# A transformer block in front of a PEER block on one core: six instead of four blocks of queries taken from the unscaled sum, and three smaller moves in the order of work

## The chip, the core and the metric

The kernel runs on one core of a Trainium2 chip. The core has five engines with a queue of instructions each: TensorE (PE in the profile; its weight loads are PEld), VectorE (DVE), ScalarE (ACT), GpSimd (POOL) and SyncE (SP), which here only starts DMA transfers. They wait for each other through semaphores. The metric is device time in microseconds (us) of one execution. A difference under about 0.2% (2.8 us) can't be told from none.

## The reference

Two layers follow each other on 256 tokens of width 1024. The first has latent attention (8 heads), differential attention (4 heads, two softmax maps each, o1 - lambda * o2, normed) and a gated FFN. The second is modulated by a condition vector: pooling and attention over neighbours and a context, then a product-key expert layer (PEER). The parts around the change, cut down:

```python
o_diff = rmsnorm(o1 - lam * o2, diff_subln_g) * (1.0 - lambda_init)     # end of differential attention
...
hx = rmsnorm(x, norm1_g) * (1 + sc1) + sh1                              # h1: x is the first layer's output xb
zx = hx @ w_in                                                          # pooled part, queries, keys, values
x = x + g1 * (concat([pool_x, attn_x], -1) @ w_out)                     # x3; w_out is wo2 in the kernel
h2 = rmsnorm(x, norm2_g) * (1 + sc2) + sh2
q = (h2 @ w_q).reshape(tokens, 8 heads, 2, 128)                         # 16 blocks of 128 query columns
s = einsum('thpd,hpnd->thpn', q, sub_keys)                              # scores against 128 keys per half
sv, si = top_k(s, 16)                                                   # and the 16 best of 16 x 16 sums
a = gelu(h2 @ u.T at the chosen experts);  x = x + g2 * ((softmax * a) @ v)
```

All 16384 experts' products are computed densely and masked; the result is within float32 accuracy.

## The kernel before

Activations lie transposed: 128 columns of the width on the partitions, 256 tokens in the free dimension, 8 such pieces (k) for the width of 1024. To keep float32 accuracy at the speed of the fast float32 format, every operand is split in a high part, rounded (`...h`, `whi`, made by ACT at L133), and the rest (`...l`, `wlo`, made by DVE at L130). A product of a weight block with the activations (`mm3`, L166) is then, for each k, three matmuls: whi x high (L169), whi x low (L170), wlo x high (L171). A block of 128 output columns with K = 8 has 24 matmuls of 128 x 256. `Weights` loads 2048 columns of weights at a time (`raw`, three buffers, SP queue) and splits 1024 columns, one block, at a time (`whi` and `wlo`, three buffers each); a buffer comes free when the last matmul that reads it has run. `lin_t` runs over the output blocks and hands the accumulators (PSUM tiles psa to psd, two buffers each) to a function that empties them.

A scheduler orders each engine's instructions when the program is built: it takes an instruction that is ready by its own timing model, the earliest in program order first, `tc.high_priority()` ahead of others, and `tc.issue_after(x)` not before x. The engines then keep this order.

The places that matter here, in order of time:

- **Differential attention** (two passes of 128 queries, qb = 0 and 1) ends with sums, a norm and the split into `odh`, `odl` (L580, L581), which the branch product wbd reads.
- **h1** (`modulated`, L660): rows of the norm (`rb`) come by a matmul broadcast (`rows_of`, L255); for each k DVE multiplies (L662, tile mdt), ACT adds the shift and rounds (L664, L668 and L133), and DVE takes the rest (L665, L130). Then `xb`, the first layer's normed output, is formed in place from x2 by eight DVE rows (L726), behind the instruction that `modulated` returns.
- **wo2** (L827): 8 blocks read `cath`, `catl`, whose pieces 0 to 3 come from the pooling and 4 to 7 from the neighbour attention's last queries.
- **The queries of PEER.** The norm of x3 needs all of x3. So `put_x3` also stores x3 times the gain unscaled (`z3`, in the tiles kall0 and kall1, with two columns of the shift behind the 256 tokens, hence 128 x 258), and the first four of the 16 blocks of wq (accumulators `psz`, two psa and two psb) are multiplied from z3; the norm's factor and the shift are applied when they are emptied (`put_pq`, L885, L886, with `rb4s`, an SBUF copy of the factor's row, and the shift's product in `sh4`). Between them stand the sum of squares (L246), GpSimd's power -1/2 (L215), the broadcast (L255) and `modulated` for h2. The other 12 blocks are multiplied from h2.
- **The search.** Each pair of query blocks is multiplied with the keys (L893), copied (`sc`, L895), and searched on DVE (`top16`, L873 to L877, and the sums' search); after all heads of 128 tokens the indices are picked out (tile eq, L955 to L967). All this is issued in pieces (`feed`) beside the dense product of h2 with u (`u_pass`), whose weight blocks need their wlo from the same DVE queue.

```python
psz = [f()[:, :S + 2] for f in (ps_a, ps_a, ps_b, ps_b)]
mm3(psz[0], wq, 0, KD, z3)
with tc.high_priority(), tc.issue_after(last_mm[0].ins):
    y4 = rsqrt_cols(ss3.done(), 1.0 / D)
mm3(psz[1], wq, KD, KD, z3)
with tc.high_priority(), tc.issue_after(last_mm[0].ins):
    rb4 = rows_of(y4)
    modulated(x3, rb4, gs2, lambda k: mod[:, 24 + k:25 + k], h2h, h2l)
for i in (2, 3):
    with tc.issue_after(last_bc[0].ins):
        mm3(psz[i], wq, i * KD, KD, z3)
```

Of the kernel before, what the change touches and what calls it, by code (L numbers as in the profile page):

```python
# [63 lines left out]
def block_kernel(ctx: ExitStack, tc: tile.TileContext, a: dict, out: bass.AP, dbg=None):  # L64
# [19 lines left out]
    def ps_a(name="psa"):  # L84
        return bank("a", name)
# [46 lines left out]
    def split(dst_h, dst_l, src, eng="v"):  # L132
        nc.scalar.activation(dst_h, src, AF.Copy)  # L133
        sub(eng, dst_l, src, dst_h)
# [28 lines left out]
            o = b % 8 * P  # L163
            return self.hl[0][:, o:o + n * P], self.hl[1][:, o:o + n * P]

    def mm3(ps, w, b, K, xs):  # L166
        for k in range(K):
            wh, wl = w(b + k)
            nc.tensor.matmul(ps, wh, xs[0][:, k], start=(k == 0), stop=False)  # L169
            nc.tensor.matmul(ps, wh, xs[1][:, k], start=False, stop=False)  # L170
            last_mm[0] = nc.tensor.matmul(ps, wl, xs[0][:, k], start=False, stop=(k == K - 1))  # L171
# [350 lines left out]
    def pv(pts, vh, o):  # L522
        for kb, p_ in enumerate(pts):
            nc.tensor.matmul(o, p_, vh(kb), start=(kb == 0), stop=(kb == len(pts) - 1))
# [28 lines left out]
    for qb in range(2):  # L553
        o1, o2 = ps_d(), ps_d()
        z = small.tile([P, 4, 2], F32, tag="dz", name="dz")
        for h0 in (0, 2):
            for e, o in enumerate((o1, o2)):
                ptss = soft([[(dq[64 * e:64 * e + 64, h], dk[64 * e:64 * e + 64, h])] for h in (h0, h0 + 1)], qb,
                            [z[:, h, e:e + 1] for h in (h0, h0 + 1)])
                for h, pts in zip((h0, h0 + 1), ptss):  # L560
                    pv(pts, lambda kb: dv[:, kb, h * 128:(h + 1) * 128], o[:, h * 128:(h + 1) * 128])
        r = small.tile([P, 4, 2], F32, tag="dr", name="dr")
        nc.vector.reciprocal(r, z)
        nc.vector.tensor_scalar(r[:, :, 1], r[:, :, 1], nlam, None, op0=OP.mult)
# [14 lines left out]
        oh, ol = (x[:, :, qb * P:(qb + 1) * P] for x in (odh, odl))  # L579
        nc.scalar.activation(oh, pv_, AF.Copy, scale=subg)  # L580
        nc.vector.scalar_tensor_tensor(ol, pv_, subg, oh.bitcast(F32), op0=OP.mult, op1=OP.subtract)  # L581

    st1a.close()

# [74 lines left out]
    def modulated(src, rb, gs, sh, hi, lo):  # L659
        for k in range(KD):  # L660
            t = mdp.tile([P, S], F32, tag="mdt", name="mdt")
            nc.vector.scalar_tensor_tensor(t, src[:, k], gs[:, k:k + 1], rb, op0=OP.mult, op1=OP.mult)  # L662
            if k % 2 == 0:
                nc.scalar.activation(hi[:, k], t, AF.Identity, bias=sh(k))  # L664
                end = nc.vector.scalar_tensor_tensor(lo[:, k], t, sh(k), hi[:, k].bitcast(F32),  # L665
                                                     op0=OP.add, op1=OP.subtract)
            else:
                nc.scalar.activation(t, t, AF.Identity, bias=sh(k))  # L668
                split(hi[:, k], lo[:, k], t)
        return end  # L670


# [151 lines left out]
        nc.vector.scalar_tensor_tensor(zl, x3[:, k], g, zh.bitcast(F32), op0=OP.mult, op1=OP.subtract)  # L824
        ss3.add(x3[:, k])

    lin_t(a["wo2"], 8, KD, (cath, catl), put_x3, grp=1)  # L827
    tap("x3", x3)
    shift = mod[:, 24:32, None].to_broadcast([P, KD, 2])
    split(z3[0][:, :, S:], z3[1][:, :, S:], shift)  # L830
    wq = Weights(a["wq"])
    psz = [f()[:, :S + 2] for f in (ps_a, ps_a, ps_b, ps_b)]

    h2h = acts.tile([P, KD, S], F32R, tag="acth", name="h2h")
    h2l = acts.tile([P, KD, S], F32R, tag="actl", name="h2l")
# [1 line left out]
    with tc.high_priority(), tc.issue_after(last_mm[0].ins):  # L837
        y4 = rsqrt_cols(ss3.done(), 1.0 / D)
    mm3(psz[1], wq, KD, KD, z3)
    with tc.high_priority(), tc.issue_after(last_mm[0].ins):  # L840
        rb4 = rows_of(y4)
        modulated(x3, rb4, gs2, lambda k: mod[:, 24 + k:25 + k], h2h, h2l)
    for i in (2, 3):
        with tc.issue_after(last_bc[0].ins):
            mm3(psz[i], wq, i * KD, KD, z3)
    h2 = (h2h, h2l)
# [31 lines left out]

    def put_pq(h2_, n, ps):
        pq = tk.tile([P, 2, S], F32, tag="pq", bufs=3, name="pq")  # L880
        if h2_ < 4:
            for i in range(2):
                z_ = psz[h2_ + i]
                nc.scalar.activation(sh4[:, h2_ + i:h2_ + i + 1], z_[:, S:S + 1], AF.Copy)
# [150 lines left out]

    rb4s = tk.tile([P, S], F32, name="rb4s")
    nc.scalar.activation(rb4s, rb4, AF.Copy)
    sh4 = tk.tile([P, 4], F32, name="sh4")
    for j in (0, 2):
        put_pq(j, 2, None)  # L1040
    lin_t(a["wq"], 16, KD, h2, put_pq, w=wq, j0=4)

    def u_pass(q):
        w = Weights(a["uT"][:, q * QJ * D:(q + 1) * QJ * D])
# [235 lines left out]
```

## Time and profile before

| | |
|---|---|
| median of 3 runs | 1380.24 us (1377.74 to 1380.52) |
| the profiled execution | 1381.32 us, of which its span 1379.1 us |
| PE, PEld | 98%, 91% of the span busy |
| DVE, ACT, POOL | 73%, 51%, 1% |
| mean granted TensorE clock | 0.994 of full speed |
| DMA | 217 GB/s over the span |

The span runs from the first to the last instruction of the profile. The busy share is time in which an engine ran at least one instruction; where an engine is nearly always busy, the little that it waits is what the order of work can still change.

### The profile page before, as it was taken

To read this page: it belongs to the slowest core of one execution; us is meant where nothing else is said; L and a number is where in the kernel's file an instruction comes from. 1 tells how busy PE (TensorE), PEld (TensorE's weight loads), DVE (VectorE), ACT (ScalarE), POOL (GpSimd) and SP (SyncE) were. 2 spreads that over 40 slices of the span, in tenths; PEclk is the share of its full clock that TensorE was granted. 3 is DMA by queue.
4 is the path that set the end of the run, shared out by engine and by line. 5 is a ranking of instruction groups with operands and counts; after the bars stand their busy time and mean duration, and the time that the engine had idled before them with its cause. 6 is when DMAs were issued, how large, how long until landed. Compare 5 with 4: busy or idle time off the path is not lost.

```text
span 1379.1 us, 24018 instructions
## 1 busy us (share of the span) xinstructions
PE 1349.9 (98%) x9736; PEld 1255.9 (91%) x9736; DVE 1013.3 (73%) x1746; ACT 708.1 (51%) x1034; POOL 20.0 (1%) x23
## 2 busy tenths in 40 slices
PE   7999999999999999899999999999999999999997
PEld 7988999999998888899999999999998888888886
DVE  5897679997988556699994998844466666677675
ACT  5564645454546555545454555544444554454443
POOL 0000000000000001000000000000000000000000
PEclk9999999999999999999999999999999999999999
DMA  6474348877885622354555678775566776778772
GB/s 238 150 249 152 107 139 298 282 275 259 284 312 203 217 93 81 138 180 158 182 196 181 238 272 296 291 274 200 196 231 228 242 250 237 263 271 285 242 236 87
DMA packets 82093, 300.44 MB, mean 218 GB/s; under 512 B 5824, under 2 KB 39232, under 8 KB 52800
## 3 DMA queue, kind: packets, MB, share of 16 engines
q1 hardware_dynamic: 76224, 274.02, 57.5%
q10 hardware_dynamic: 5760, 24.91, 4.5%
q8 instruction: 76, 1.25, 0.3%
q14 instruction: 33, 0.27, 0.1%
HBM read 276.88 MB, written 22.02 MB: 217 GB/s over the span
## 4 chain that ended last, share of the span: by engine, by line
PE 89%; DVE 5%; DMA 3%; issue 2%; ACT 1%; POOL 0%; SPq 0%; POOLq 0%; DVEq 0%; ACTq 0%
PE acc L1096 25%; PE psc L169 9%; PE psc L171 9%; PE psc L170 9%; PE psa L170 8%; PE psa L171 8%; PE psa L169 8%; DMA aw<-in_ada 3%; DVE wlo L130 2%; PE psd L1012 1%; PE psb L1012 1%; PE psd L774 1%; PE psb L505 1%; PE psb L762 1%; DVE jk L304 1%
## 5 line engine op out<-in xcount | busy, mean ns | idle before, releaser
L133 ACT ACTIVATE whi<-raw 128x1024 fp32r<-128x1024 f32 (+1 forms) x426 | 448.4, 1053 | 491.5 <-PE psc L170 176.2
L130 DVE TENSOR_TENSOR wlo<-raw,whi 128x1024 fp32r<-128x1024 f32 (+1 forms) x426 | 518.3, 1219 | 217.3 <-ACT whi L133 216.2
L169 PE MATMUL psc<-h2h,whi 128*128 128x256 f32 x1024 | 290.9, 284 | 0.0
L171 PE MATMUL psc<-h2h,wlo 128*128 128x256 f32 x1024 | 289.8, 284 | 0.0
L170 PE MATMUL psc<-h2l,whi 128*128 128x256 f32 x1024 | 289.6, 283 | 0.0
L170 PEld LDWEIGHTS psc<-h2l,whi 128*128 128x128 f32 x1024 | 196.4, 192 | 0.0
L169 PEld LDWEIGHTS psc<-h2h,whi 128*128 128x128 f32 x1024 | 196.3, 192 | 0.0
L171 PEld LDWEIGHTS psc<-h2h,wlo 128*128 128x128 f32 x1024 | 196.1, 192 | 0.0
L1096 PE MATMUL acc<-wlo,wgh 128*128 128x512 f32 x512 | 159.9, 392 | 0.8 <-DVE wlo L130 0.8
L1096 PE MATMUL acc<-whi,wgl 128*128 128x512 f32 x512 | 158.9, 389 | 0.0
L1096 PE MATMUL acc<-whi,wgh 128*128 128x512 f32 x512 | 139.6, 390 | 0.0
L1096 PEld LDWEIGHTS acc<-whi,wgl 128*128 128x128 f32 x512 | 96.1, 188 | 20.1
L1096 PEld LDWEIGHTS acc<-whi,wgh 128*128 128x128 f32 x512 | 95.8, 188 | 20.2 <-ACT whi L133 0.2
L1096 PEld LDWEIGHTS acc<-wlo,wgh 128*128 128x128 f32 x512 | 95.1, 188 | 20.4 <-DVE wlo L130 1.1
L171 PE MATMUL psa<-acth,wlo 128*128 128x256 f32 x352 | 99.8, 284 | 0.6 <-DVE wlo L130 0.6
L169 PE MATMUL psa<-acth,whi 128*128 128x256 f32 x352 | 99.8, 283 | 0.1
L170 PE MATMUL psa<-actl,whi 128*128 128x256 f32 x352 | 99.6, 283 | 0.0
L169 PE MATMUL psa<-xh,whi 128*128 128x256 f32 x240 | 70.9, 295 | 7.1 <-ACT whi L133 6.4
L170 PE MATMUL psa<-xl,whi 128*128 128x256 f32 x240 | 70.9, 296 | 0.7 <-DVE xl L332 0.7
L171 PE MATMUL psa<-xh,wlo 128*128 128x256 f32 x240 | 70.9, 296 | 0.0
L171 PEld LDWEIGHTS psa<-acth,wlo 128*128 128x128 f32 x352 | 67.6, 192 | 0.8 <-DVE wlo L130 0.8
L169 PEld LDWEIGHTS psa<-acth,whi 128*128 128x128 f32 x352 | 67.6, 192 | 0.3 <-DVE xT L614 0.3
(416 smaller groups left out, 2437.9 us busy)
## 6 DMA issues: line engine op xcount, KB each, us to landing
raw<-in_uT SPq DMA_DIRECT2D x64, 1024.0 KB, 4.9
raw<-in_v SPq DMA_DIRECT2D x64, 1024.0 KB, 4.9
aw<-in_ada SPq DMA_DIRECT2D x48, 512.0 KB, 5.8
raw<-in_wgu SPq DMA_DIRECT2D x22, 1024.0 KB, 4.8
ggd<-gs ACTq DMA_DIRECT2D x16, 1024.0 KB, 5.2
gh<-ggd SPq DMA_DIRECT2D x16, 1024.0 KB, 8.1
raw<-in_wA SPq DMA_DIRECT2D x14, 1024.0 KB, 4.9
raw<-in_wdn SPq DMA_DIRECT2D x11, 1024.0 KB, 7.2
```

The lines of the kernel that those rows point to most:

```text
L130: e.tensor_tensor(dst, src, hi.bitcast(F32), op=OP.subtract)
L133: nc.scalar.activation(dst_h, src, AF.Copy)
L169: nc.tensor.matmul(ps, wh, xs[0][:, k], start=(k == 0), stop=False)
L170: nc.tensor.matmul(ps, wh, xs[1][:, k], start=False, stop=False)
L171: last_mm[0] = nc.tensor.matmul(ps, wl, xs[0][:, k], start=False, stop=(k == K - 1))
L304: nc.vector.scalar_tensor_tensor(jk, aw, 1.0, c_, op0=OP.mult, op1=OP.mult, accum_out=dst[:, t:t + 1])
L505: nc.tensor.matmul(s[:, i], q_[:, qb * P:(qb + 1) * P], k_[:, :n], start=(j == 0), stop=False)
L762: nc.tensor.matmul(s, q2[x_][hd, hp, qs_], kall[y_][hd, hp], start=(i == 0), stop=(i == 2))
L774: nc.tensor.matmul(o[:, h * 64:(h + 1) * 64], pts[:, kb * P:(kb + 1) * P], v2[:, kb, h * 64:(h + 1) * 64], start=(kb == 0), stop=(kb == 3))
L1012: nc.tensor.matmul(ps[:, t4 * P:(t4 + 1) * P], o1[:, 2 * g4 + t4 // 2, :, t4 % 2], og[:, c, 2 * g4 + t4 // 2, :, t4 % 2], start=(c == 1), ...
L1096: r = nc.tensor.matmul(acc[tt][n], x_, w_[:, n * 512:(n + 1) * 512], start=st, stop=sp)
```

## The change

Four moves:

1. Six blocks of wq, not four, are multiplied from z3 (`NZ = 6`, the two more in psc buffers), so ten are left for h2. Half of block 2 (k = 0 to 3) is issued before the broadcast, the other half and blocks 3 to 5 behind it.
2. `modulated` returns the last low half of k = 7 instead of that of k = 6, so what is placed behind it (xb) stands behind all of h1. Its odd pieces are written out, with the same operations as `split`.
3. wo2's first two blocks are issued as k = 0 to 3 of both, then k = 4 to 7 of both.
4. The end of differential attention for qb = 1 is issued under `tc.high_priority()`.

```diff
+    def held(w, b):
+        hi, lo = w(b, 8)
+        return lambda c: (hi[:, (c - b) * P:(c - b + 1) * P], lo[:, (c - b) * P:(c - b + 1) * P])
+
-    def mm3(ps, w, b, K, xs):
-        for k in range(K):
+    def mm3(ps, w, b, K, xs, ks=None):
+        for k in ks or range(K):
...
+        hurry = ExitStack()
+        if qb == 1:
+            hurry.enter_context(tc.high_priority())
         r = small.tile([P, 4, 2], F32, tag="dr", name="dr")
...
         nc.vector.scalar_tensor_tensor(ol, pv_, subg, oh.bitcast(F32), op0=OP.mult, op1=OP.subtract)
+        hurry.close()
...
-                end = nc.vector.scalar_tensor_tensor(lo[:, k], t, sh(k), hi[:, k].bitcast(F32),
-                                                     op0=OP.add, op1=OP.subtract)
+                nc.vector.scalar_tensor_tensor(lo[:, k], t, sh(k), hi[:, k].bitcast(F32),
+                                               op0=OP.add, op1=OP.subtract)
             else:
                 nc.scalar.activation(t, t, AF.Identity, bias=sh(k))
-                split(hi[:, k], lo[:, k], t)
+                nc.scalar.activation(hi[:, k], t, AF.Copy)
+                end = nc.vector.tensor_tensor(lo[:, k], t, hi[:, k].bitcast(F32), op=OP.subtract)
...
-    lin_t(a["wo2"], 8, KD, (cath, catl), put_x3, grp=1)
+    wo2 = Weights(a["wo2"])
+    first = [(ps_a(), held(wo2, j * KD), j) for j in range(2)]
+    for ks in (range(4), range(4, KD)):
+        for ps, w_, j in first:
+            mm3(ps[:, :S], w_, j * KD, KD, (cath, catl), ks)
+    for ps, _, j in first:
+        put_x3(j, 1, ps[:, None, :S])
+    lin_t(a["wo2"], 8, KD, (cath, catl), put_x3, grp=1, w=wo2, j0=2)
...
-    psz = [f()[:, :S + 2] for f in (ps_a, ps_a, ps_b, ps_b)]
+    NZ = 6
+    psz = [f()[:, :S + 2] for f in (ps_a, ps_a, ps_b, ps_b, ps_c, ps_c)]
...
-    with tc.high_priority(), tc.issue_after(last_mm[0].ins):
+    mm3(psz[2], wq, 2 * KD, KD, z3, range(4))
+    end = last_mm[0]
+    with tc.high_priority(), tc.issue_after(end.ins):
         rb4 = rows_of(y4)
         modulated(x3, rb4, gs2, lambda k: mod[:, 24 + k:25 + k], h2h, h2l)
-    for i in (2, 3):
+    with tc.issue_after(last_bc[0].ins):
+        mm3(psz[2], wq, 2 * KD, KD, z3, range(4, KD))
+    for i in range(3, NZ):
         with tc.issue_after(last_bc[0].ins):
             mm3(psz[i], wq, i * KD, KD, z3)
...
-        if h2_ < 4:
+        if h2_ < NZ:
...
-    for j in (0, 2):
+    for j in range(0, NZ, 2):
         put_pq(j, 2, None)
-    lin_t(a["wq"], 16, KD, h2, put_pq, w=wq, j0=4)
+    lin_t(a["wq"], 16, KD, h2, put_pq, w=wq, j0=NZ)
```

What the scheduler makes of it is seen in the order of each engine's instructions. On PE, around the sum of squares of x3 (psd_5996) and the broadcast of its root (ny), before (psb_6287 is the accumulator of block 2):

```order
L246 MATMUL psd_5996<-cst_76,sq_6281 128x1
L170 MATMUL psa_6286<-kall1_4832,whi_6329 128x258
L171 MATMUL psa_6286<-kall0_4831,wlo_6330 128x258
L255 MATMUL psd_6357<-cst_76,ny_6325 128x128 x2
L169 MATMUL psb_6287<-kall0_4831,whi_6398 128x258
L170 MATMUL psb_6287<-kall1_4832,whi_6398 128x258
L171 MATMUL psb_6287<-kall0_4831,wlo_6399 128x258
```

and in the changed program, where L251 is the sum, L260 the broadcast, L174 to L176 the three matmuls, and the "..." stands for nine more rows of psb_6287:

```order
L251 MATMUL psd_5996<-cst_76,sq_6281 128x1
L175 MATMUL psa_6286<-kall1_4832,whi_6331 128x258
L176 MATMUL psa_6286<-kall0_4831,wlo_6332 128x258
L174 MATMUL psb_6287<-kall0_4831,whi_6361 128x258
L175 MATMUL psb_6287<-kall1_4832,whi_6361 128x258
L176 MATMUL psb_6287<-kall0_4831,wlo_6362 128x258
...
L260 MATMUL psd_6377<-cst_76,ny_6327 128x128 x2
```

Twelve matmuls of block 2 moved ahead of the broadcast. Behind it stand the other twelve, then 24 each into psb_6288, psc_6289 and psc_6290, and then the first matmul on h2h.

On DVE at the end of h1, before (h1l is the low half of h1, xT holds x2 and then xb, wlo_5163, wlo_5191 and wlo_5224 belong to the first three blocks that are multiplied with h1):

```order
L665 SCALAR_TENSOR_TENSOR h1l_5101<-mdt_5129,mod_79,h1h_5100 128x256
L726 SCALAR_TENSOR_TENSOR xT_75<-xT_75,cols_73,rbf_5141 128x256 x4
L130 TENSOR_TENSOR h1l_5101<-mdt_5124,h1h_5100 128x256
L726 SCALAR_TENSOR_TENSOR xT_75<-xT_75,cols_73,rbf_5141 128x256 x4
L130 TENSOR_TENSOR wlo_5191<-raw_5160,whi_5190 128x1024
L130 TENSOR_TENSOR h1l_5101<-mdt_5133,h1h_5100 128x256
L130 TENSOR_TENSOR wlo_5224<-raw_5221,whi_5223 128x1024
```

and in the changed program:

```order
L674 SCALAR_TENSOR_TENSOR h1l_5101<-mdt_5129,mod_79,h1h_5100 128x256
L679 TENSOR_TENSOR h1l_5101<-mdt_5124,h1h_5100 128x256
L130 TENSOR_TENSOR wlo_5191<-raw_5160,whi_5190 128x1024
L679 TENSOR_TENSOR h1l_5101<-mdt_5133,h1h_5100 128x256
L736 SCALAR_TENSOR_TENSOR xT_75<-xT_75,cols_73,rbf_5141 128x256 x8
L130 TENSOR_TENSOR wlo_5224<-raw_5221,whi_5223 128x1024
```

The eight rows of xb moved behind the last two low halves and ahead of wlo_5224.

On DVE in the first `u_pass`, beside the search, before (eq picks indices; wlo_7556 is the low half of the weight block that PE takes at 658 us of the profile):

```order
L130 TENSOR_TENSOR wlo_7507<-raw_7476,whi_7506 128x1024
L950 TENSOR_TENSOR ij_7541<-ijt_7542 128x128
L960 TENSOR_TENSOR eq_7549<-eq_7549,sf_7473 128x2048
L876 MAX sv_8067<-s2_8068 128x8
L876 MAX sv_8067<-s2_8074 128x8
L874 MAX_INDEX ti_7756<-tv_7755,cd_7997 128x8
L875 MATCH_REPLACE cd2_7998<-tv_7755,cd_7997 128x80
L874 MAX_INDEX si_7757<-sv_8150,sc4_6483 128x8 x2
L130 TENSOR_TENSOR wlo_7556<-raw_7553,whi_7555 128x1024
```

and in the changed program, where the same block's low half is wlo_7562:

```order
L130 TENSOR_TENSOR wlo_7513<-raw_7482,whi_7512 128x1024
L897 MATCH_REPLACE s2_8074<-sv_8073,sc3_6542 128x128
L897 MATCH_REPLACE s2_8080<-sv_8073,sc3_6542 128x128
L895 MAX tv_7761<-cd_8003 128x8
L895 MAX sv_8156<-sc4_6543 128x8 x2
L899 MAX_INDEX ti_7762<-tv_7761,cd2_7921 128x8
L972 TENSOR_TENSOR ij_7547<-ijt_7548 128x128
L982 TENSOR_TENSOR eq_7555<-eq_7555,sf_7479 128x2048
L130 TENSOR_TENSOR wlo_7562<-raw_7559,whi_7561 128x1024
```

The six short rows between eq and the low half moved behind it; and over the whole stretch from the first row of the search (MAX of sc0) to this low half the changed queue holds two rows of L130 fewer, since two more blocks of wq are split before the search begins. For moves 3 and 4 the rows of all engines stand as before, apart from line numbers and buffer numbers. On SP one load of w2 stands ahead of that of row_icnt, the counts of the pooling, no longer behind it.

## Rows read from the trace of the kernel before

**Rows 1.** The page, busy time, share of the span and instructions of each engine.

```profile
PE 1349.9 (98%) x9736; PEld 1255.9 (91%) x9736; DVE 1013.3 (73%) x1746; ACT 708.1 (51%) x1034; POOL 20.0 (1%) x23
```

**Rows 2.** Timeline of PE, pauses: start, us, instruction, idle before, releaser.

```profile
183.20 0.50 PE L169 MATMUL psa<-odh,whi 128*128 128x256 f32 x2 [1.22 <-ACT odh L580]
184.54 0.39 PE L170 MATMUL psa<-odl,whi 128*128 128x256 f32 x1 [0.84 <-DVE odl L581]
...
446.60 0.39 PE L170 MATMUL psa<-h1l,whi 128*128 128x256 f32 x1 [1.21 <-DVE h1l L130]
...
563.15 0.71 PE L255 MATMUL psd<-cst,ny 128*128 128x128 f32 x4 [1.78 <-POOL ny L215]
...
574.56 0.35 PE L169 MATMUL psa<-h2h,whi 128*128 128x256 f32 x1 [3.44 <-DVE pq L885]
```

**Rows 3.** Stretches: length, busy time of each engine, granted clock, DMA share, GB/s.

```profile
core 0 of [0], span 1379.1 us
...
182.00:188.00 6.00, 3.96 (x23) 3.76 (x24) 2.16 (x3) 1.14 (x2) 0.00 (x0) 0.82 0.51 175
446.00:450.00 4.00, 3.40 (x28) 3.40 (x29) 2.91 (x4) 1.17 (x2) 0.00 (x0) 1.00 0.99 373
562.00:566.00 4.00, 2.85 (x19) 2.85 (x20) 3.77 (x8) 2.04 (x6) 1.09 (x1) 0.84 0.63 209
566.00:570.00 4.00, 4.00 (x28) 4.00 (x28) 2.27 (x5) 1.93 (x6) 0.00 (x0) 0.74 0.13 53
574.00:578.00 4.00, 3.44 (x17) 3.47 (x18) 1.94 (x7) 1.71 (x4) 0.00 (x0) 0.62 0.13 53
578.00:582.00 4.00, 4.00 (x36) 4.00 (x35) 1.28 (x10) 1.62 (x3) 0.00 (x0) 0.96 0.01 4
588.00:594.00 6.00, 6.00 (x53) 6.00 (x52) 6.00 (x32) 2.90 (x4) 0.00 (x0) 1.00 0.60 214
```

**Rows 4.** Timeline of PE, blocks 2 and 3 from the unscaled sum.

```profile
565.07 0.42 PE L170 MATMUL psb<-kall,whi 128*128 128x258 f32 x1
...
567.64 0.42 PE L170 MATMUL psb<-kall,whi 128*128 128x258 f32 x1
...
568.22 0.28 PE L170 MATMUL psb<-kall,whi 128*128 128x258 f32 x1
...
570.84 0.28 PE L171 MATMUL psb<-kall,wlo 128*128 128x258 f32 x1
```

**Rows 5.** Timeline of DVE and ACT between the broadcast and the first scores.

```profile
563.90 1.66 DVE L662 SCALAR_TENSOR_TENSOR mdt<-xT,gs,psd 128x256 f32<-128x256 f32 x4 [0.23 <-PE psd L255]
...
568.10 1.06 ACT L133 ACTIVATE whi<-raw 128x1024 fp32r<-128x1024 f32 x1 [2.07 <-PE psb L170]
...
573.15 0.37 ACT L1037 ACTIVATE rb4s<-psd 128x256 f32<-128x256 f32 x1
...
574.00 0.75 DVE L885 TENSOR_TENSOR pq<-psa,rb4s 128x256 f32<-128x256 f32 x2
...
580.09 0.60 ACT L895 ACTIVATE sc<-psd 128x512 f32<-128x512 f32 x1 [3.93 <-PE psd L893]
...
580.72 0.49 DVE L873 MAX8 sv<-sc 128x8 f32<-128x128 f32 x2 [4.78 <-ACT sc L895]
```

**Rows 6.** Timeline of PE and DVE at the end of h1.

```profile
442.25 0.39 PE L169 MATMUL psa<-h1h,whi 128*128 128x256 f32 x1
...
443.41 1.67 DVE L726 SCALAR_TENSOR_TENSOR xT<-xT,cols,rbf 128x256 f32<-128x256 f32 x4
...
446.12 0.42 DVE L130 TENSOR_TENSOR h1l<-mdt,h1h 128x256 fp32r<-128x256 f32 x1
446.46 1.23 DVE L130 TENSOR_TENSOR wlo<-raw,whi 128x1024 fp32r<-128x1024 f32 x1
```

**Rows 7.** Timeline of DVE and PE in the first dense pass.

```profile
653.41 2.29 DVE L960 TENSOR_TENSOR eq<-eq,sf 128x2048 f16<-128x2048 f16 x1
...
656.96 2.34 DVE L130 TENSOR_TENSOR wlo<-raw,whi 128x1024 fp32r<-128x1024 f32 x2
...
658.17 0.44 PE L171 MATMUL psc<-h2h,wlo 128*128 128x256 f32 x2
```

More of the change, by code (lines that the diff above doesn't have):

```diff
@@ L1037, in block_kernel @@
     nc.scalar.activation(rb4s, rb4, AF.Copy)
-    sh4 = tk.tile([P, 4], F32, name="sh4")
-    for j in (0, 2):
+    sh4 = tk.tile([P, NZ], F32, name="sh4")
+    for j in range(0, NZ, 2):
         put_pq(j, 2, None)
-    lin_t(a["wq"], 16, KD, h2, put_pq, w=wq, j0=4)
+    lin_t(a["wq"], 16, KD, h2, put_pq, w=wq, j0=NZ)
     def u_pass(q):
```

## The prediction

> **What bounds the kernel now.** I read the page first, then what TensorE waited for in order of time, then the clock by stretches, and last what the two engines that feed TensorE do where it waits. TensorE (PE) is busy for 1349.9 us of the span of 1379.1 us [rows 1, 3], so a change can give back only PE's pauses and the time at the lower clock. The pauses are few. Three belong to the places that the change touches: 1.21 us at 446.60, 1.78 us at 563.15, 3.44 us at 574.56; two more, 1.22 and 0.84 us, stand at the end of differential attention, at 183.20 and 184.54 [rows 2]. The clock costs as well. After the pauses at 563 and 574 the granted clock falls from 1.00 to means of 0.84, 0.74 and 0.62, 0.96 [rows 3], that is to the lower of its two levels (1.2 GHz) for (0.16 + 0.26) x 4 / 0.5 = 3.4 us each time; around the 1.21 us at 446.60 it stays at 1.00 [rows 3]. In such a stretch the matmuls start 0.214 us apart (12 steps from 565.07 to 567.64), outside it 0.119 us (22 steps from 568.22 to 570.84) [rows 4]. So 3.4 us at 1.2 GHz does the work of 1.9 us and loses 1.5 us.
>
> Why PE waits at 563 to 574: the squares of x3 are summed, GpSimd makes the root (PE waits 1.78 us for it), the broadcast follows, and then VectorE (DVE) and ScalarE (ACT) make h2 from 563.90 on. PE has only two blocks of wq from the unscaled sum to do meanwhile. It ends them at 571.1 and then stands before the first matmul on h2, which writes a psa buffer that still holds block 0; DVE frees it with the products at 574.00, and these follow ACT's copy of the row at 573.15 [rows 5].
>
> **Part 1, six blocks from the unscaled sum.** GpSimd's result does not come earlier, so the broadcast stays at 563.15. Before it stand now 12 matmuls of block 2: 12 x 0.119 = 1.43 us of the 1.78 us are filled, and 0.35 us of pause are left. That is far under the 1.21 us that kept the clock, so I count no lower clock at 564.7. The broadcast's four records take 0.47 us; after it stand the other 12 matmuls of block 2 and 24 each of blocks 3, 4 and 5: 84 x 0.119 = 10.0 us, until 573.6. The first h2 matmul (now of block 6) stands there. Is it ready? ACT's conversion of the weights of block 5 needs the buffers of block 2; it ran at 568.10 after 2.07 us of waiting, since block 2 fell into the slow stretch [rows 5], and runs at about 565.2 now. The chain through h2 keeps its operations (some 0.4 us each on DVE and ACT) and gets one more conversion in the middle: 1.06 us on ACT [rows 5], 1.17 on DVE [rows 7]. From 563.90 I add on DVE: four products to 565.5, one low half, a wait for block 5's high half to 566.3, its split to 567.5, eight operations to 570.2, block 6's split to 571.3, three low halves to 572.4, then the product that frees psa at 572.8. On ACT the row's copy ends at 571.5. So 573.6 stands with 0.8 us to spare, and no pause is left; without one the clock should hold too.
>
> The gain: PE starts at 573.6 instead of 574.56 (0.96 us), has two blocks fewer to do from there (48 x 0.119 = 5.7 us), and loses no 1.5 us to the clock behind it. Sum 8.1 us. Bounds: if h2 came 3.44 us late again, 8.1 - 3.4 - 1.5 = 3.2 us remain; if the 0.35 us vanished too, 8.5.
>
> The added blocks' evacuation (a product on DVE, of which two take 0.75 us at 574.00 [rows 5], and two short rows on ACT, per block, in place of half an ACT copy) lies in time in which PE works on h2 blocks; that is its cover.
>
> **What is late next.** Behind 574 DVE has the top-16 search of all heads and the low halves of PE's weights in one queue, and it is full: 6.00 of 6.00 us between 588 and 594, with PE at 6.00 too [rows 3]. It starts with the first scores, at 580.72; these wait for ACT's copy at 580.09, 5.5 us after PE's first h2 matmul, 1.5 of them owed to the clock [rows 5]. Now that is 573.6 + 4.0 + 0.6 = 578.3: 2.4 us earlier, while PE is 8.1 us earlier. The low half with the least to spare against PE is the one behind the product eq (2.29 us at 653.41): it ended at 656.96 + 1.17 = 658.1, and PE took it at 658.17 or just behind [rows 7]. Up to that split the new DVE order holds the same search work less six short rows (the pair of MAX8 at 580.72 takes 0.49 us [rows 5]: 0.24 x 6 = 1.4 us) and two low halves less, since two blocks of wq came before the search began (2 x 1.17 [rows 7] = 2.3 us). DVE is there 2.4 + 1.4 + 2.3 = 6.1 us earlier; PE wants it 8.1 us earlier and had 0.1 to 0.2 us to spare: PE waits about **1.9 us**. Bounds: 0 if the search starts 1.9 us sooner than I add up, 3.5 if the first scores come only 0.8 us sooner, not 2.4. I take 1.9. Once PE has waited there, the later splits have that much more room.
>
> Here a rule of the Trainium skill can be weighed. The row: PE stood 3.44 us before one matmul [rows 2], and no matmul from behind it ran meanwhile. The skill's page "TensorE: Matmul & The Clock Gate", section "Architectural detail", says that VectorE's and ScalarE's queues are strictly first in, first out, and that TensorE only pulls weight loads ahead. By that rule a late low half holds back all of PE, and the 1.9 us are paid in full; could PE step past it, the sum would be 1.9 us better. The trace agrees with the rule, by the 3.44 us.
>
> **Part 2, the end of h1 ahead of xb.** DVE now does the last two low halves of h1 before the eight rows of xb. These eight (four take 1.67 us at 443.41, four more stand before them; 0.4 us from one start to the next) stood ahead of the last low half, at 446.12 [rows 6]: it ends 3.15 us sooner, at 443.4. PE's first h1 matmul starts at 442.25 [rows 6] and wants it 22 matmuls on, at 444.9. So the 1.21 us pause goes. Late next is the low half of the next block, still at 446.46, ending 447.6 [rows 6]: PE wants it 50 matmuls on, at 448.2. Gain **1.2 us** (bounds 0.6, if that split is another 0.6 us late, and 1.2).
>
> **Parts 3 and 4, wo2's halves and the priority in differential attention.** On every engine the rows of the changed program stand in these two places as before. I cost both at nothing: the 1.22 and 0.84 us at 183 to 185 stay, and so does the lower clock behind them (0.82 between 182 and 188 [rows 2, 3]). On SP's queue one load of w2 goes ahead of the row of counts, which is read only after the second attention's last keys and values are projected; that stage covers it.
>
> **Sum.** 8.1 - 1.9 + 1.2 = 7.4 us. The profiled execution took 1381.32 us, its span 1379.1, so 2.2 lie around it; with the change 1373.9. It stands 1.1 us over the median of the runs shown, 1380.24, so the median should be 1372.8.
>
> **Rivals.**
> - *The lo splits are in time.* For it: my sum for DVE leans on one step of 0.1 to 0.2 us. Against: DVE shows no idle time there. 9.3 us gained: 1370.9.
> - *The late split costs the clock too.* PE's pause is then like the 1.78 us one that brought 1.2 GHz for 3.4 us: 7.4 - 1.5 = 5.9, and with a pause of 3.5 us 4.3: 1374.3 to 1375.9. Against: the pause may stay under what the 1.21 us row shows to be harmless.
> - *DVE becomes the pace of the whole search* (slower than before from a point). From 578 to about 686 its queue is full, 108 us in which PE now runs ahead of it. Each per cent that these rows take longer than before costs 1.08 us. From 4.3% on the gain is under 2.8 us, at 6.9% it is gone, from 9.4% on the kernel is slower by over 0.2%; at 10%, 1383.6. For it: no idle time in [rows 3]. Against: no row of the search changes its shape.
> - *The change does what it says in parts 3 and 4 too.* Then the 2.06 us at 183 to 185 and 1.5 us of clock would go: 1369.2. Against: no row there has moved.
>
> **Chances.** Forecast 0.46 (own range 1371.7 to 1373.9), splits in time 0.17, clock too 0.21, DVE as the pace up to no gain 0.09 and beyond 0.04, parts 3 and 4 0.03. About 0.2% (2.8 us) is what a measurement of this kernel tells from no change, and the runs shown spread over as much. Faster 0.87, same 0.09, slower 0.04. The range runs from the splits in time, with 1 us for that spread, to the clock case: 1369.8 to 1376.2.
>
> **What would show it.** Right: no pause over 0.5 us at 563 and none at 574; clock 1.00 from 558 to 582; the 446.60 row without a pause; the pauses at 183 as before; one wait of PE for a low half (L130) of 1 to 3 us near 650. Wrong: a wait of PE for h2 or psa at 573; waits for low halves all along 590 to 690; a new stretch at 1.2 GHz.

## The result, and the profile after

| | median of its runs | median of the kernel before beside it | ratio, 95% interval |
|---|---|---|---|
| changed kernel | 1371.24 us (1366.81 to 1373.68, 6 runs) | 1378.99 us (6 runs) | 0.9941 (0.9926 to 0.9956) |

7.75 us less, by the interval 6.1 to 10.2. The prediction said 1372.8, faster: right in sign and inside its range. The profiled execution took 1370.94 us with a span of 1369.0. The page's busy times:

```profile
PE 1345.6 (98%) x9736; PEld 1252.0 (91%) x9736; DVE 1012.5 (74%) x1748; ACT 708.7 (52%) x1037; POOL 20.2 (1%) x23
```

PE does the same 9736 instructions in 4.3 us less busy time [rows 1]; less time at the lower clock is a part of it. Where it waits, from the timeline of PE of the changed kernel (start, us, instruction, idle before, releaser; rows without brackets had no pause and mark a place):

```profile
180.76 0.50 PE L174 MATMUL psa<-odh,whi 128*128 128x256 f32 x2 [1.22 <-ACT odh L588]
182.11 0.39 PE L175 MATMUL psa<-odl,whi 128*128 128x256 f32 x1 [0.84 <-DVE odl L589]
...
439.62 0.39 PE L174 MATMUL psa<-h1h,whi 128*128 128x256 f32 x1
...
524.02 0.39 PE L174 MATMUL psa<-cath,whi 128*128 128x256 f32 x1
...
528.63 0.66 PE L792 MATMUL psc<-cst,non 128*128 128x128 f32 x4 [0.61 <-DVE non L789]
529.98 0.51 PE L174 MATMUL psa<-cath,whi 128*128 128x256 f32 x2 [0.69 <-ACT cath L133]
530.70 0.41 PE L175 MATMUL psa<-catl,whi 128*128 128x256 f32 x1 [0.22 <-DVE catl L130]
...
560.57 0.71 PE L260 MATMUL psd<-cst,ny 128*128 128x128 f32 x4 [0.32 <-POOL ny L220]
...
571.21 0.28 PE L174 MATMUL psa<-h2h,whi 128*128 128x256 f32 x1
...
648.12 0.39 PE L176 MATMUL psc<-h2h,wlo 128*128 128x256 f32 x1 [0.32 <-DVE wlo L130]
...
1354.32 0.50 PE L1118 MATMUL acc<-wlo,wgh 128*128 128x512 f32 x1 [0.77 <-DVE wlo L130]
```

Of [rows 2], the pauses at the end of h1 and before h2 are gone, the one before the broadcast is 0.32 us instead of 1.78, and the two at the end of differential attention stand as they were. Two more places of the kernel before are needed to lay the two traces over each other, the first row of wo2 and the last products:

```profile
528.11 0.39 PE L169 MATMUL psa<-cath,whi 128*128 128x256 f32 x1
...
1364.43 0.50 PE L1096 MATMUL acc<-wlo,wgh 128*128 128x512 f32 x1 [0.77 <-DVE wlo L130]
```

The clock, from stretches of the changed kernel (length, busy time of each engine, granted clock, DMA share, GB/s):

```profile
182.00:188.00 6.00, 5.89 (x36) 5.89 (x37) 1.36 (x4) 1.06 (x1) 0.00 (x0) 0.72 0.13 53
530.00:534.00 4.00, 3.78 (x18) 3.57 (x19) 1.13 (x2) 0.93 (x1) 0.00 (x0) 0.62 0.00 0
534.00:538.00 4.00, 4.00 (x34) 4.00 (x34) 3.85 (x7) 2.85 (x7) 0.00 (x0) 0.96 0.41 111
562.00:582.00 20.00, 20.00 (x171) 20.00 (x170) 18.48 (x62) 15.68 (x33) 0.00 (x0) 1.00 0.47 164
575.81:647.97 72.16, 71.98 (x605) 71.78 (x603) 72.16 (x343) 38.53 (x47) 0.00 (x0) 1.00 0.47 164
```

Between 562 and 582 the clock is 1.00 throughout, where [rows 3] had 0.84, 0.74, 0.62 and 0.96. Behind wo2's pauses there is a stretch at 1.2 GHz (0.62) that the execution of before had not.

Where the time came from is read best between places that both traces have. In us, from the profiled execution of each kernel, the experiments included: from the first matmul on h1h to the first on cath; to the broadcast of x3's root; to the first matmul on h2h; to the wait among the last products.

| | h1 to wo2 | to the broadcast | to h2 | to the last products |
|---|---|---|---|---|
| before | 85.86 | 35.04 | 11.41 | 789.87 |
| changed | 84.40 | 36.55 | 10.64 | 783.11 |
| part 1 alone | 85.85 | 36.55 | 10.62 | 783.10 |
| part 2 alone | 84.40 | 35.03 | 11.44 | 790.84 |
| parts 3, 4 alone | 85.86 | 35.03 | 11.44 | 791.06 |
| six, no half ahead | 84.40 | 36.33 | 13.61 | 784.28 |
| four, half ahead | 84.39 | 36.80 | 9.83 | 790.64 |
| search 2.7 us later | 84.39 | 35.30 | 10.60 | 782.87 |
| the same, held | 84.40 | 35.03 | 10.65 | 788.17 |
| search 10.9 us longer | 84.39 | 36.28 | 10.60 | 782.55 |
| wbm's last block late | 84.39 | 36.64 | 10.65 | 783.13 |
| three blocks of wo2 | 84.40 | 32.26 | 10.83 | 783.20 |
| both covers | 84.42 | 32.27 | 10.83 | 783.23 |

So the changed rows took 1.46 (h1) + 0.77 + 6.76 = 9.0 us less. The stretch at wo2, whose rows didn't change, took 1.5 us more (the clock). The remaining 2.6 us of the 10.1 us between the two spans lie ahead of h1's first matmul (442.25 [rows 6] against 439.62), where the rows read the same too. That is the execution, not the change: in the kernels of the table with the same rows up to there, h1's first matmul comes at 437.2 to 444.1 us.

### The profile page after: what moved, and what is told of

It is laid out like the page before. It is cut to its first block, busy times and chain, and to the rows that moved or that the text cites. A ratio compares the mean times of both kernels' runs of the same rounds, so it can differ in the third digit from the quotient of the medians.

```text
span 1369.0 us, 24025 instructions
## 1 busy us (share of the span) xinstructions
PE 1345.6 (98%) x9736; PEld 1252.0 (91%) x9736; DVE 1012.5 (74%) x1748; ACT 708.7 (52%) x1037; POOL 20.2 (1%) x23
## 4 chain that ended last, share of the span: by engine, by line
PE 88%; DVE 7%; DMA 2%; issue 1%; ACT 1%; POOL 0%; ACTq 0%; POOLq 0%; SPq 0%; DVEq 0%
PE acc L1118 25%; PE psa L175 9%; PE psa L174 9%; PE psa L176 9%; PE psc L174 8%; PE psc L176 8%; PE psc L175 8%; DVE wlo L130 3%; DMA aw<-in_ada 2%; PE psd L1034 1%; PE psb L1034 1%; PE psd L784 1%; PE psb L510 1%; PE psb L772 1%; PE psa L205 1%
## 5 line engine op out<-in xcount | busy, mean ns | idle before, releaser
L130 DVE TENSOR_TENSOR wlo<-raw,whi 128x1024 fp32r<-128x1024 f32 (+1 forms) x426 | 517.7, 1217 | 213.5 <-ACT whi L133 212.2
L174 PE MATMUL psc<-h2h,whi 128*128 128x256 f32 x1024 | 290.8, 284 | 0.0
L176 PE MATMUL psc<-h2h,wlo 128*128 128x256 f32 x1024 | 289.9, 284 | 0.3 <-DVE wlo L130 0.3
L176 PEld LDWEIGHTS psc<-h2h,wlo 128*128 128x128 f32 x1024 | 196.0, 192 | 0.5 <-DVE wlo L130 0.5
L174 PEld LDWEIGHTS psc<-h2h,whi 128*128 128x128 f32 x1024 | 196.3, 192 | 0.0
L174 PE MATMUL psa<-acth,whi 128*128 128x256 f32 x352 | 99.9, 284 | 1.2 <-DVE ft L651 0.6
L176 PE MATMUL psa<-acth,wlo 128*128 128x256 f32 x352 | 99.8, 284 | 0.6 <-DVE wlo L130 0.6
L174 PE MATMUL psa<-xh,whi 128*128 128x256 f32 x240 | 69.9, 291 | 7.0 <-ACT whi L133 6.6
L176 PE MATMUL psa<-xh,wlo 128*128 128x256 f32 x240 | 69.9, 291 | 0.0
L174 PEld LDWEIGHTS psa<-acth,whi 128*128 128x128 f32 x352 | 67.6, 192 | 1.6 <-DVE xT L623 0.8
L176 PEld LDWEIGHTS psa<-acth,wlo 128*128 128x128 f32 x352 | 67.6, 192 | 0.8 <-DVE wlo L130 0.8
```

The costliest lines, as they stand in the source:

```text
L130: e.tensor_tensor(dst, src, hi.bitcast(F32), op=OP.subtract)
```

## Experiments

**Part 1 alone.** Against the changed kernel, with `modulated`, wo2 and differential attention as before:

```diff
...
-        hurry = ExitStack()
...
-                nc.scalar.activation(hi[:, k], t, AF.Copy)
-                end = nc.vector.tensor_tensor(lo[:, k], t, hi[:, k].bitcast(F32), op=OP.subtract)
+                split(hi[:, k], lo[:, k], t)
...
-    for ks in (range(4), range(4, KD)):
...
+    lin_t(a["wo2"], 8, KD, (cath, catl), put_x3, grp=1)
...
```

> Part 1 alone (six blocks from the unscaled sum, half of block 2 ahead of the broadcast), the other three parts as before. Theory (each part removes its own pause and nothing else): first h2 matmul without a pause and no 1.2 GHz stretch between 558 and 582, two blocks fewer behind it, one wait of about 0.3 us near 650: 7.5 to 8 us less than before; the 1.2 us pause at the end of h1 stays. Rival (a good part of the measured gain is owed to the other parts or to a lucky start of the execution): 5 us less or still smaller.

Measured: 1370.68 us, ratio 0.9938 (0.9918 to 0.9957) to 1379.80. Its stretches to h2 and behind it are those of the changed kernel to 0.02 us, with the same 0.32 us waits at 559.55 and 647.07. Part 1 is most of the change: 0.8 + 6.8 of the 9.0 us by the table.

**Part 2 alone.** The edit of `modulated` on the kernel before:

```diff
...
-                split(hi[:, k], lo[:, k], t)
+                nc.scalar.activation(hi[:, k], t, AF.Copy)
+                end = nc.vector.tensor_tensor(lo[:, k], t, hi[:, k].bitcast(F32), op=OP.subtract)
```

> Part 2 alone (xb behind all of h1). Theory: the pause of 1.2 us at the end of h1 goes and 1.2 us are gained, the most that a single pause without a lower clock can give; in the profile the time from the first h1 matmul to the row nt of x3's norm, 118.8 us before, becomes 117.6. Rival (the time is given back at wo2, since the last heads of neighbour attention wait for DVE and ACT and not for TensorE): the stretch stays at 118.8 and the time as before.

Measured: 1378.05 us, ratio 0.9991 (0.9978 to 1.0005): too small for the measurement of the whole, but the stretch from h1 to wo2 is 84.40 instead of 85.86, and the next one is not longer. The 1.46 us are not given back. This execution also shows what the pause before h2 may cost. From its timeline and stretches:

```profile
569.88 0.55 PE L169 MATMUL psa<-h2h,whi 128*128 128x256 f32 x1 [3.45 <-DVE pq L886]
```

```profile
566.00:570.00 4.00, 0.55 (x5) 0.38 (x3) 3.84 (x10) 3.09 (x9) 0.00 (x0) 0.82 0.72 262
570.00:574.00 4.00, 4.00 (x19) 4.00 (x20) 1.27 (x5) 1.48 (x4) 0.00 (x0) 0.50 0.00 0
574.00:578.00 4.00, 4.00 (x31) 4.00 (x30) 0.99 (x8) 1.33 (x3) 0.00 (x0) 0.82 0.02 4
```

That is (0.18 + 0.50 + 0.18) x 4 / 0.5 = 6.9 us at 1.2 GHz, of which 1.3 still lie in the pause (1.4 up to 570, less the 0.1 behind 569.88) and 5.5 in work, where [rows 3] have 3.4 us behind the same pause. So the kernel before loses 1.5 us there in one execution and about 1 us more in another (790.84 and 791.06 against 789.87), and part 1 removes both.

**Parts 3 and 4 alone**, on the kernel before:

```diff
+        if qb == 1:
+            hurry.enter_context(tc.high_priority())
...
+    for ks in (range(4), range(4, KD)):
+        for ps, w_, j in first:
+            mm3(ps[:, :S], w_, j * KD, KD, (cath, catl), ks)
...
```

> Parts 3 and 4 alone (wo2's first two blocks in halves, priority at the end of differential attention). Theory: every engine's instructions stand in the same order as before, so the time is as before within 1 us, with the pauses of 1.22 and 0.84 us behind the transposes of od and of 0.6, 0.7 and 0.2 us at wo2. Rival (they work as their text says): 3.5 us less, both sets of pauses gone.

Measured: 1381.30 us, ratio 1.0010 (0.9997 to 1.0024): no gain. All five engines hold the same rows in the same order as before, and the pauses are there to 0.01 us:

```profile
181.36 0.50 PE L174 MATMUL psa<-odh,whi 128*128 128x256 f32 x2 [1.22 <-ACT odh L588]
182.71 0.39 PE L175 MATMUL psa<-odl,whi 128*128 128x256 f32 x1 [0.84 <-DVE odl L589]
```

**Six blocks, none of block 2 ahead of the broadcast.** Against the changed kernel:

```diff
-    mm3(psz[2], wq, 2 * KD, KD, z3, range(4))
...
-        mm3(psz[2], wq, 2 * KD, KD, z3, range(4, KD))
-    for i in range(3, NZ):
+    for i in range(2, NZ):
```

> The changed kernel, but with all of block 2 behind the broadcast: six blocks, nothing to fill the wait for GpSimd's root. Theory (pause and clock are paid by themselves): the pause before the broadcast is 1.8 us again and the granted clock falls behind it, so 1.4 + 1.5 = 2.9 us of part 1's gain are lost: about 5 us less than before, 2.9 more than the changed kernel. Rival (the chain through h2 on DVE and ACT is what ends last, so PE may as well wait at the broadcast): as the changed kernel, 7.7 us less than before.

Measured: 1375.14 us, ratio 0.9952 (0.9934 to 0.9970), 3.9 us over the changed kernel's median. To h2 it takes 13.61 us instead of 10.64: 2.97 us, as worked out. The rest is a new wait in the dense pass:

```profile
561.83 0.90 PE L260 MATMUL psd<-cst,ny 128*128 128x128 f32 x4 [1.78 <-POOL ny L220]
...
653.51 0.39 PE L174 MATMUL psc<-h2h,whi 128*128 128x256 f32 x1 [1.52 <-ACT ga L1068]
```

The clock fell behind the broadcast, as expected:

```profile
562.00:566.00 4.00, 4.00 (x22) 4.00 (x23) 3.58 (x10) 1.61 (x4) 0.00 (x0) 0.57 0.73 262
```

At 653.51 PE waits for a psc buffer that ACT's gelu frees. The gelu isn't late: it starts 77.44 us behind the first h2 matmul, in the changed kernel 77.47. It is PE's order that differs. In this program the first two matmuls of a later block, which need that buffer, stand directly behind the pair of blocks that the gelu empties; in the changed program 24 matmuls of another block stand between. So the different rows around the broadcast led to another order on PE 90 us later.

**Four blocks, half of block 2 ahead.** Against the changed kernel:

```diff
-    NZ = 6
-    psz = [f()[:, :S + 2] for f in (ps_a, ps_a, ps_b, ps_b, ps_c, ps_c)]
+    NZ = 4
+    psz = [f()[:, :S + 2] for f in (ps_a, ps_a, ps_b, ps_b)]
```

> The changed kernel with four blocks from the unscaled sum as before, half of block 2 ahead of the broadcast. Theory (the added blocks as cover carry most of the gain): the pause before the broadcast is filled, but the one before the first h2 matmul grows to 4 to 5 us, since PE comes there earlier and the chain through h2 doesn't, and the granted clock falls behind it; 1 to 3.5 us less than before with the 1.2 us of part 2 in it. Rival (filling the wait for the root and keeping the clock is what counts): 5 us less or better.

Measured: 1377.05 us, ratio 0.9976 (0.9966 to 0.9986):

```profile
559.87 0.71 PE L260 MATMUL psd<-cst,ny 128*128 128x128 f32 x4 [0.32 <-POOL ny L220]
...
569.70 0.55 PE L174 MATMUL psa<-h2h,whi 128*128 128x256 f32 x1 [4.79 <-DVE pq L907]
```

```profile
562.00 1.06 ACT L133 ACTIVATE whi<-raw 128x1024 fp32r<-128x1024 f32 x1 [0.37 <-PE psb L175]
```

The filled pause moved to h2: the two pauses are 0.32 and 4.79 us, together 5.1, where they were 1.78 and 3.44, together 5.2. Still h2 comes 9.83 us behind the broadcast instead of 11.41, 1.6 us sooner: ACT's conversion waits only 0.37 us for block 2, which PE now ends sooner and at a granted clock of 1.00 (562 to 566), instead of 2.07 [rows 5]. Behind h2 790.64 us are to go, as before. So the half alone is worth 1.6 us, and 3 us once the two added blocks are there; these carry most of the gain.

**The search 2.7 us later.** The prediction held that DVE's queue has no room up to the low half behind eq, and the changed kernel does wait there (0.32 us). Four rows more at the start of the search, with an unused result:

```diff
...
+        for _ in range(4):
+            nc.vector.max(spare, scs[0].rearrange("p i n -> p (i n)"))
         for tt in range(2):
```

> The changed kernel with four more MAX8 rows over 512 elements on DVE at the start of the search (some 2.2 us, their result is not used). Theory (DVE's queue is full up to the low half behind the product eq, and PE waits there already): PE's wait near 648 us grows from 0.32 us to about 2.5 us, and the time by 2.2 us, or by 3.7 us if the wait also costs the clock. Rival (PE is ahead of DVE nowhere else and the queue has slack): under 0.5 us more than the changed kernel.

Measured: 1369.81 us, ratio 0.9930 (0.9916 to 0.9943): nothing lost, and PE shows no wait near 650. The rows took 0.69 us each. The theory fell, as stated. The timeline of DVE tells why:

```profile
642.24 1.21 DVE L130 TENSOR_TENSOR wlo<-raw,whi 128x1024 fp32r<-128x1024 f32 x1
...
646.04 1.20 DVE L130 TENSOR_TENSOR wlo<-raw,whi 128x1024 fp32r<-128x1024 f32 x1
...
647.58 2.28 DVE L986 TENSOR_TENSOR eq<-eq,sf 128x2048 f16<-128x2048 f16 x1
```

The low half that PE waits for in the changed kernel is here the one at 642.24; PE takes it 2.5 us after its end. With more work in the search the scheduler put it, and the next one, ahead of eq. What there was to spare was not in DVE's queue but in the order.

**The same, with the low half held behind eq:**

```diff
...
-                    split(hi[:, o:o + step], lo[:, o:o + step], r[:, o:o + step], lo_eng.next())
+                    nc.scalar.activation(hi[:, o:o + step], r[:, o:o + step], AF.Copy)
+                    with tc.issue_after(behind.pop().ins) if behind else nullcontext():
+                        sub(lo_eng.next(), lo[:, o:o + step], r[:, o:o + step], hi[:, o:o + step])
...
+                if tt == 0 and p_ == 0:
+                    behind.append(picked)
```

> The kernel with four more MAX8 rows at the start of the search, with the low half of the next weights held behind the product eq, where it stands in the changed kernel. Theory (what saved the run with four rows was only that this low half moved ahead of eq): PE waits 2 to 4.5 us for it between 640 and 650, and the time is longer by as much, or by 1.5 us more with the clock. Rival (DVE had more room there than the changed kernel's 0.32 us wait tells): no wait over 1 us, the time as with the four rows alone.

Measured: 1377.08 us, ratio 0.9972 (0.9958 to 0.9987), by the medians 7.3 us and behind h2, where the hold acts, 5.3 us more than without it (788.17 against 782.87). Two low halves stand behind eq now, and PE waits:

```profile
649.64 0.39 PE L177 MATMUL psc<-h2h,whi 128*128 128x256 f32 x1 [1.28 <-ACT ga L1081]
651.07 0.38 PE L179 MATMUL psc<-h2h,wlo 128*128 128x256 f32 x1 [0.93 <-DVE wlo L130]
...
660.08 0.38 PE L179 MATMUL psc<-h2h,wlo 128*128 128x256 f32 x1 [0.35 <-DVE wlo L130]
...
671.20 0.39 PE L179 MATMUL psc<-h2h,wlo 128*128 128x256 f32 x1 [1.55 <-DVE wlo L130]
```

```profile
640.00:680.00 40.00, 35.73 (x289) 34.67 (x288) 40.00 (x154) 15.60 (x21) 0.00 (x0) 1.00 0.41 147
```

4.1 us in four waits. A late low half is paid, as the theory says; it is spread over later blocks, not one pause as expected. The wait for ACT's gelu ahead of it adds nothing of its own, since the low half ends only at 651.02. The listed pauses are short of the 5.3 us because a pause is listed from the end of the matmul ahead of it, and in a row without pauses the next one starts before that end. Counted from start to start, against the usual 0.119 us, the four and a fifth of 0.16 us at 666.53 take 5.6 us, and 0.3 us of such steps are there without the hold too: that is the 5.3. The clock stayed at 1.00, so this loss is of pauses alone.

**The search 10.9 us longer.** One more row for each head and token half:

```diff
...
+                nc.vector.max(spare, scs[h].rearrange("p i n -> p (i n)"))
                 yield
```

> The changed kernel with one more MAX8 over 512 elements for each head of both token halves, 16 in all at 0.69 us, 11 us or 10% of the 108 us in which DVE's queue is full; their result is not used. The rival that the prediction priced (DVE becomes the pace, 1.08 us for each per cent): 11 us slower than the changed kernel, some 1382. Theory after the run with four such rows (the low halves are put ahead of the search, which only ends later): no pause of PE over 0.5 us in the first dense pass, within 1.5 us of the changed kernel.

Measured: 1369.79 us, ratio 0.9925 (0.9907 to 0.9943). From the groups of DVE's rows (line, operation, count, busy us, mean ns, idle before):

```profile
L936 DVE MAX8 spare<-sc 128x8 f32<-128x512 f32 x16 | 10.9, 684 | 0.0
```

With 10.9 us of search added, PE has no pause of 0.2 us or more between the broadcast and the last products, and the stretch behind h2 is 782.55. The search's last row ends 135.0 us behind the first h2 matmul instead of 118.2. For rows that the scheduler places itself, the rival "DVE becomes the pace" is refuted up to 10%. Rows that take longer in an order that stays weren't tried; the run with the hold shows what a fixed place can cost.

**What parts 3 and 4 would be worth.** Their text didn't move a row, so two kernels put rows where PE waits. First, the last block of wbm, 12 matmuls, behind the transposes of od:

```diff
...
+    mm3(bm[:, :S], wbm, 6 * 4, 4, (omh, oml))
+    with tc.issue_after(od_end.ins):
+        mm3(bm[:, S:], wbm, 7 * 4, 4, (omh, oml))
...
```

> The changed kernel with the last block of wbm (12 matmuls) issued behind the transposes of od, so that PE has 1.4 us of work there. Theory: the pauses of 1.22 and 0.84 us behind the transposes shrink to 0.6 us or less in sum and the 1.2 GHz stretch at 183 goes: 3 to 3.5 us less than the changed kernel, 11 less than before. Rival (the transposes, now 1.4 us earlier, wait for od instead, or ACT's conversion of the next weights stands ahead of odh): the pause only moves, no gain.

Measured: 1366.91 us, ratio 0.9911 (0.9896 to 0.9926), 4.3 us under the changed kernel's median. From PE's timeline (no brackets, no pause) and a stretch:

```profile
177.71 0.66 PE L585 MATMUL psc<-cst,od 128*128 128x128 f32 x4
...
179.63 0.28 PE L174 MATMUL psa<-odh,whi 128*128 128x256 f32 x1
```

```profile
182.00:188.00 6.00, 6.00 (x52) 6.00 (x52) 4.95 (x8) 2.75 (x3) 0.00 (x0) 1.00 0.38 127
```

Both pauses and the 0.72 are gone.

Second, the first halves of three blocks of wo2, one behind the last head's product, one behind its transposes:

```diff
...
+    first = [(f(), held(wo2, j * KD), j) for j, f in enumerate((ps_a, ps_a, ps_b))]
+    for (ps, w_, j), late in zip(first, (None, pv_end, cat_end)):
+        with tc.issue_after(late.ins) if late else nullcontext():
+            mm3(ps[:, :S], w_, j * KD, KD, (cath, catl), range(4))
...
```

> The changed kernel with the first halves of three blocks of wo2 instead of two, the second behind the last head's product, the third behind the last transposes. Theory: the pauses of 0.61, 0.69 and 0.22 us at wo2 go, and with them the 1.2 GHz stretch that the changed kernel's profile shows there: 1.5 to 3 us less than the changed kernel. Rival (the chain of the last head ends last whatever PE does meanwhile): the waits stay, no gain.

Measured: 1367.89 us, ratio 0.9905 (0.9891 to 0.9920). From wo2's first row to the broadcast it takes 32.26 us instead of 36.55 (or 35.03 where the clock held). The timeline of PE there has no pause left; the 12 matmuls of the third block fill the wait for cath:

```profile
529.96 0.36 PE L174 MATMUL psb<-cath,whi 128*128 128x256 f32 x1
...
531.46 0.40 PE L174 MATMUL psa<-cath,whi 128*128 128x256 f32 x2
```

**Both covers** (the two diffs together):

> The changed kernel with both covers together: the last block of wbm behind the transposes of od, and the first halves of three blocks of wo2. Theory (the two places are independent, each gives its own pauses and its own clock back): the times add up, 2.1 to 3.5 us at 180 and 2.8 to 4.3 us at 525, so 5 to 8 us less than the changed kernel and 13 to 15 less than before, with no pause over 0.7 us between 30 us and the last products. Rival (PE comes earlier to a later stage that DVE or DMA sets, and waits there): 10 us less than before or worse, with a new wait in the dense passes.

Measured: 1363.57 us, ratio 0.9884 (0.9865 to 0.9903): 7.7 us under the changed kernel's median, faster than both kernels of this study. The gains nearly add up (0.0030 and 0.0036 of the time, together 0.0057; by the medians 4.3 and 3.4 us, together 7.7). Nothing new waits behind them. One pause of 1.77 us at 232 us, in the gated FFN, varies from execution to execution with the same rows (from under 0.2 to 2.2 us), so the expectation of no pause over 0.7 us was too bold. The wait near 650 is as in the changed kernel:

```profile
642.65 0.39 PE L176 MATMUL psc<-h2h,wlo 128*128 128x256 f32 x1 [0.35 <-DVE wlo L130]
```

## Why the prediction was right, and where it was off

- **The wait at the broadcast.** 0.35 us forecast, 0.32 measured, and no lower clock behind it. Six blocks without the half show both prices: 2.97 us for 1.43 + 1.5.
- **The first h2 matmul.** Forecast 10.45 us behind the broadcast without a pause; it came at 10.64, without one. The chain through h2 was added up well: the product that frees psa was forecast 9.65 us behind the broadcast, and its pair starts at 569.84, 9.3 us behind it, with the first of the two done about 0.4 us later.
- **Behind h2.** Forecast: 5.7 us for two blocks, 1.5 for the clock, less 1.9 for the late low half, 5.3 us. Measured: 6.76 us. The step that was mis-sized is the **1.9 us**: PE waited at the named place, for the named low half, but 0.32 us. From the timeline of DVE of the changed kernel:

```profile
569.84 0.74 DVE L907 TENSOR_TENSOR pq<-psa,rb4s 128x256 f32<-128x256 f32 x2
...
575.81 0.49 DVE L895 MAX8 sv<-sc 128x8 f32<-128x128 f32 x2 [1.09 <-ACT sc L917]
...
644.63 2.29 DVE L982 TENSOR_TENSOR eq<-eq,sf 128x2048 f16<-128x2048 f16 x1
646.83 1.23 DVE L130 TENSOR_TENSOR wlo<-raw,whi 128x1024 fp32r<-128x1024 f32 x1
```

  Measured from the broadcast, the search starts 2.3 us sooner (15.24 us behind it, before 17.57), as forecast (2.4). From that start to the end of that low half DVE took 72.16 us; before it took this (stretch of the kernel before):

```profile
580.72:658.09 77.37, 77.37 (x652) 77.37 (x651) 76.95 (x355) 40.45 (x48) 0.00 (x0) 1.00 0.47 164
```

  That is 5.2 us less, not 3.7. Both counted terms hold. Two low halves, 1.13 us each from start to start, are 2.3 us, and the six short rows took 1.35 us in the kernel before, from 655.61 to 656.96 [rows 7]:

```profile
655.61 0.49 DVE L876 MAX8 sv<-s 128x8 f32<-128x128 f32 x2
```

  The other 1.6 us are time that the order before lost between rows of the search, and that the prediction put at nothing. By the order of the built program, eight rows of this stretch read exactly what the row right ahead of them has written. They start 0.25 to 0.28 us behind it, as in this pair of the kernel before:

```profile
607.17 0.22 DVE L916 TENSOR_SCALAR cd<-sv 128x16 f32<-128x16 f32 x1
607.42 0.24 DVE L873 MAX8 tv<-cd 128x8 f32<-128x80 f32 x1
```

  In the changed kernel's order no row of the stretch does so, and rows of the same kinds are 0.12 to 0.16 us apart. Here the MAX8 reads another buffer than the one just written:

```profile
590.83 0.22 DVE L938 TENSOR_SCALAR cd<-sv 128x16 f32<-128x16 f32 x1
590.95 0.24 DVE L898 MAX8 tv<-cd 128x8 f32<-128x80 f32 x1
```

  The eight rows are 1.1 of the 1.6 us; the rest are delays that I can't assign, and no run tests either by itself. So DVE was there 7.5 us earlier and PE 7.8. The case that came about is nearly the rival "the lo splits are in time" (1370.9; chance 0.17), not the likeliest.
- **A late low half holds back PE.** In the run with the hold, ACT had made the high halves by 646.2, but DVE took the low ones only behind eq, at 649.79, and PE waited. The rule that the prediction weighed, strictly first in, first out for VectorE (the Trainium skill, "TensorE: Matmul & The Clock Gate", section "Architectural detail"), agrees with that.
- **The end of h1.** Forecast 1.2, the upper of its two bounds; measured 1.46 in the stretch, and no other wait took its place. The price was too low because the listed 1.21 us run from the end of the matmul ahead:

```profile
445.11 0.28 PE L169 MATMUL psa<-h1h,whi 128*128 128x256 f32 x1
```

  From its start to that of the row behind the pause, 446.60 [rows 2], it is 1.49 us, where a step without a pause takes 0.12; the next step takes 0.1 us more than usual too.
- **Parts 3 and 4.** Nothing forecast, nothing measured, and the reason holds: no row moved. The kernel with both covers shows that some 7.7 us lay there.
- **The rivals.** No clock was lost at the late split: its pause was short, and in the run with the hold pauses of 1.28 and 0.93 us close together didn't cost it either. "DVE becomes the pace" priced each per cent of search at 1.08 us. 10.9 us more rows cost nothing: the pricing assumed that the order stays as it is, but each program is ordered anew, and the low halves go ahead of the search, which only ends later.
- **The sum.** The wait at the low half, listed with 0.32, costs 0.6 us from start to start. With this in place of 1.9 and 1.46 in place of 1.2 the sum would have been 9.0 us, and the stretches say 9.0. The medians say 7.75, interval 6.1 to 10.2; the measurement can't tell 9 from 7.4. That 7.75 stands so near to 7.4 is luck: two terms were too pessimistic, by 1.6 us together, and the profiled execution lost 1.5 us at wo2 that the prediction doesn't have. Part 1 alone measured 9.1 us less than the kernel before.

## What to carry to other kernels

Where a serial chain (a norm, a broadcast, a split) keeps the matrix engine waiting, count the cover on both sides of each wait: filling one of two waits in a row moves the pause to the next, as four blocks with a half showed (1.6 us were left of it, 3 with cover on both sides). When an edit is to change an order, read the order: priority and a rewritten loop moved nothing here, while one block held back behind the right instruction gave 4 us. And an engine that is 100% busy beside the bound is not yet a bound itself if a scheduler can let its urgent rows pass: test it by adding rows, not by its busy share.

## What the runs showed of the hardware that wasn't expected

- The same rows and the same pauses don't always cost the clock (the two rows below are of the run with the search later). wo2's pauses (0.61, 0.69, 0.22 us) brought a stretch at 1.2 GHz in 6 of 11 profiled executions with the same rows there, 1.3 to 1.8 us each by the table (36.3 to 36.8 against 35.0 to 35.3). The pauses of 1.22 and 0.84 us at the end of differential attention brought one in 10 of 11, but not in the run with the search later:

```profile
182.00:188.00 6.00, 3.94 (x31) 3.52 (x29) 2.56 (x4) 1.66 (x3) 0.00 (x0) 1.00 0.48 175
...
530.00:534.00 4.00, 3.77 (x32) 3.71 (x32) 1.83 (x3) 2.21 (x4) 0.00 (x0) 1.00 0.00 0
```

  So such a pause costs the clock with some chance, and one profile can show either outcome. What decides it, these runs don't tell. At wo2 none of the three kernels without part 1 shows the stretch, and six of the eight with all or half of it do. The rows up to there are the same, but so few executions don't exclude a link to the change.
- Stretches that no edit touched repeat to 0.03 us between profiled executions (84.39 to 84.42 from h1 to wo2 in ten kernels), so differences of a tenth can be read from one profile there, though the whole time of the changed kernel spreads over 7 us. What spreads lies elsewhere: from differential attention to h1 the same rows took 255.8 to 262.1 us.
